# Turning the corner blocks of an attention on VectorE in 32x32 squares

## The chip, the core and the metric

The kernel runs on one core of one Trainium2 chip. What counts is the device time of one execution, in microseconds. Before the change the median of three runs was 533.24 us (532.93 to 533.34). A core has several engines, each with its own queue of instructions that it works through in order: TensorE (matrix products and full transposes; PE in the profile, PEld for its weight loads), VectorE (DVE), ScalarE (ACT), GpSimd (POOL) and SyncE (SP, which here only issues DMA transfers). They wait for each other through semaphores.

## The reference

One layer of an encoder on a sequence of 512 positions of 1024 numbers, all in float32. Cut to what matters:

```python
h = rms_norm(x, attn_norm_g)
xr, gate, q, k, v = split(h @ w_in)
y_rnn  = (rg_lru(conv(xr), forward) + rg_lru(conv(xr), backward)) * gelu(gate)
y_attn = dilated_attention(q, k, v, rel_bias)      # 8 heads of 64
x = x + concat(rms_norm(y_rnn), rms_norm(y_attn)) @ w_out
x = x + square(relu(rms_norm(x) @ w_up)) @ w_down  # 4096 wide
return rms_norm(x, final_norm_g)
```

The attention has three windows per head: 64 keys to each side at distance 1, 64 at distance 4 and 64 at distance 16, each key with a bias by its relative position; the three outputs are weighted by their softmax denominators, which makes it one softmax in which a key counts as often as windows hold it. A query sees keys at most 64 away if the distance is odd or even without being a multiple of four, and up to 256 or 512 away at multiples of four and sixteen. So between positions of different parity only the near keys count.

## The kernel before, in words

**Layout.** Positions are sorted by parity: 256 even ones, then 256 odd ones, in tiles of 128. A query tile needs 256 keys of its own parity and 160 of the other, 416 keys (`NK`) in one contiguous stretch of a doubled key tile `kk`. The scores of a query tile and a head stand in a buffer `e` of 128 queries by 512 columns, of which 416 are in use: columns 0 to 415 for the tiles called far, 96 to 511 for the others. So in each `e` three blocks of 128 keys are full and the fourth holds only 32 keys, those nearest to the border of the tile; the remaining 96 columns are filled with zeros (L840). Of those 32 keys only the 32 queries at that border see any; for the other 96 queries the bias drives the exponential to zero.

**The loop (L1164).** It has five turns `i` and in each four steps `u`, one for each query tile in the order `QSEQ`. Heads go in pairs `p`. In step (i, u) the engines get, in this order:

- `att_s(i, u)` (L815): the scores of pair i, four products on TensorE (L824) into two PSUM banks `ps`;
- `att_t` (L858) for both heads of pair i-1 and the key tile u: four transposes each on TensorE (L862) into a PSUM bank `pt`, then one copy by ScalarE (L864) of 416 of its columns to a buffer `ett` in SBUF. The banks `pt` and the bank `prow` below come from the same two;
- `att_e(i, u)` (L826): for each of the two heads a zero fill by GpSimd (L840), a pass of VectorE that adds the bias and finds the row's minimum (L841), and the exponential with its sum on ScalarE (L842);
- in step 0, `att_z(i-1)`: reciprocals of the sums and a copy to `z` on VectorE (L886, L888). `z` is transposed later in that step by TensorE (`att_zt`, L892, into `prow`) and copied by ScalarE (L893);
- in step 0 of the turns 2 and 4, `att_av` (L955): the products of the transposed exponentials with the values (L964) into `pav`; pair 0 in turn 2, pairs 1 and 2 in turn 4, and pair 3 behind the loop;
- pieces of other work between them: the projections of the next pair's queries and keys (`pqk`, evicted to `qraw` and `kraw`), their splits in a high and a low part (`qh`, `ql`, `kk`; L789, L797, L802), with DMA copies to the other half of the partitions (L791, L799, L803), and the first products of the output projection (`pwo`), from the queue `fillers`; `beside` holds steps at fixed places.

The order on TensorE, ScalarE, VectorE and GpSimd is the order in which the program issues, with no scheduler behind it. Buffers of 128x512 come from one pool of 45 (tag `g`); an instruction that first writes a buffer waits for the last readers of what it held. The bias tiles `tws` (tile `tw`) are loaded by DMA from DRAM two steps and more ahead, into four buffers. Products with weights are made of three passes (L317, L318, L319), of the high and low parts of both factors; ScalarE makes the high part of a weight (`whi`, L252) and VectorE the low part (`wlo`, L274).

Behind the loop come the rest of the output projection (to about 210 us), the up projection and the down projection of the MLP, and the final norm.

The lines that decide which blocks a key tile has:

```python
def blocks(jt):
    par, hj = jt // 2, jt % 2
    own = [(2 * (1 - par) + a, (P * hj if a else TH + P * hj)) for a in range(2)]
    oth = [(2 * par + a, (TH + P * hj if a else P * hj)) for a in range(2)]
    return (own + oth, slice(0, NK)) if hj else (oth + own, slice(S - NK, S))
```

Each entry is a query tile and the column of `e` at which the block of 128 keys starts. The entry whose block is nearly empty is the first for even key tiles (its keys are columns 96 to 127 of `e`), and the last for odd ones (columns 384 to 415).

Of the kernel before, what the change touches and what calls it, by code (L numbers as in the profile page):

```python
# [17 lines left out]
P = 128  # L18
S = 512
# [19 lines left out]
NK = TH + WN  # L39
# [64 lines left out]
def hybrid_kernel(ctx: ExitStack, tc, xw0, xw, xn, w_in, w_v, w_out, w_up, w_dn, gates, vecs, rel, onehot, fg, out):  # L104
    nc = tc.nc
# [12 lines left out]
    def g_(name, dt=FT, shape=(P, S)):  # L118
        return work.tile(list(shape), dt, name=name, tag="g", bufs=NG)

    def small(name, w):
        return work.tile([P, w], FT, name=name, tag="sm%d" % w, bufs=8)

    def ps_(name, tag):
        return psum.tile([P, S], FT, name=name, tag=tag, bufs={"pj": 4, "gs": 2, "et": 2}[tag])
# [361 lines left out]
    def load_tw(h, v):  # L487
        t = work.tile([P, 1024], FT, name="tw", tag="tw", bufs=4)[:, :2 * WN + TH + P]
        b = nbd.offset + h * 2 * S
        nc.sync.dma_start(t[:, WN:WN + TH + P], bass.AP(tensor=nbd.tensor, offset=b, ap=[[1, P], [1, TH + P]]))  # L490
        k = TH - WN - v
        nc.sync.dma_start(bass.AP(tensor=t.tensor, offset=t.offset, ap=[t.ap[0], [WN + TH + P, 2], [1, WN]]),
                          bass.AP(tensor=nbd.tensor, offset=b + S + k, ap=[[1, P], [P - 1 + v - k, 2], [1, WN]]))
        tws[h, v] = t
# [222 lines left out]
    for n, (k, tt) in enumerate(steps):  # L717
        c = C_V + k // 2
# [88 lines left out]
    et, en, zs = {}, {}, {}  # L807
# [7 lines left out]
    def att_s(p, u):  # L815
        qt = QSEQ[u]
        par, far = QT[qt]
        c0 = P * qt
        w = {(0, 0): TH + TH - WN, (0, 1): 0, (1, 0): TH - WN, (1, 1): TH}[par, far]
        psq[p] = [ps_("ps", "gs") for _ in range(2)]  # L820
        for e in range(2):
            k = k_tile(p, e)[:, w:w + NK]
            for i, n in enumerate(("h", "l")):
                nc.tensor.matmul(psq[p][e][:, :NK], lhsT=sp[p, 0, n, e][:, c0:c0 + P], rhs=k, start=i == 0, stop=i == 1)  # L824

    def att_e(p, u):  # L826
        qt = QSEQ[u]
        par, far = QT[qt]
        v = int(par != far)
        if u == 0:  # L830
            en[2 * p], en[2 * p + 1] = {}, {}
            zs[p] = small("zz", 8)
        pss = psq.pop(p)
        c0 = (WN + P) * far
        for e in range(2):
            h = 2 * p + e
            t = g_("e")
            mn = small("mn", 1)
            x = t[:, :NK] if far else t[:, S - NK:]
            nc.gpsimd.memset(t[:, NK:] if far else t[:, :S - NK], 0.0)  # L840
            nc.vector.tensor_tensor_reduce(x, pss[e][:, :NK], tws[h, v][:, c0:c0 + NK], 1.0, 3.0e38, OP.add, OP.min, mn)  # L841
            act(x, x, AF.Exp, scale=-1.0, bias=mn, accum_out=zs[p][:, 2 * qt + e:2 * qt + e + 1])  # L842
            en[h][qt] = t
            if u in (1, 3):
                del tws[h, v]
        if u == 3:
            for e in range(2):
                del sp[p, 0, "h", e], sp[p, 0, "l", e], sp[p, 1, "h", e]
            del kks[p]
# [7 lines that stand above are left out]

    def att_t(h, jt):  # L858
        pt = ps_("pt", "et")
        bs, c = blocks(jt)  # L860
        for i, (qt, k) in enumerate(bs):
            nc.tensor.transpose(pt[:, i * P:(i + 1) * P], en[h][qt][:, k:k + P], ident)  # L862
        t = g_("ett")
        act(t[:, c], pt[:, c], AF.Copy)  # L864
        et[h, jt] = t
        if jt == 3:
            del en[h]

# [15 lines left out]
    def att_z(p):  # L884
        rz = small("rz", 8)
        nc.vector.reciprocal(rz, zs.pop(p))  # L886
        z16[p] = g_("z16")[:, :P]
        nc.vector.tensor_copy(z16[p], fan(rz, 0, 8, 16))  # L888

    def att_zt(p):  # L890
        pr = ps_("prow", "et")
        nc.tensor.transpose(pr[:, :P], z16[p], ident)  # L892
        act(z16[p], pr[:, :P], AF.Copy)  # L893

    def att_zd(p):
        zrow[p] = g_("zrow")
        t = z16.pop(p)
        for qt in range(4):
            r = t[32 * qt:32 * qt + 32]
            nc.sync.dma_start(zrow[p][:, qt * P:(qt + 1) * P],  # L900
                              bass.AP(tensor=r.tensor, offset=r.offset, ap=[r.ap[0], [0, 4], [1, P]]))

    def att_y(p):
        y_add(1)
# [50 lines left out]
    def att_av(p, jts):  # L955
        if 0 in jts:
            pav[p] = ps_("pav", "gs" if p else "pj")
        for jt in jts:
            parts = av_parts(jt)
            for i, (ci, co) in enumerate(parts):  # L960
                for e in range(2):
                    a = slice(64 * e, 64 * e + 64)
                    h = 2 * p + e
                    nc.tensor.matmul(pav[p][a, co], lhsT=vs[:, jt, h * DH:(h + 1) * DH], rhs=et[h, jt][:, ci],  # L964
                                     start=jt == 0 and i == 0, stop=jt == 3 and i == len(parts) - 1, skip_group_check=True)
            for e in range(2):
                del et[2 * p + e, jt]
        if 3 in jts:
            y = g_("yp")
            nc.vector.tensor_tensor(y[:, ::-1], pav.pop(p), zrow.pop(p), op=OP.mult)  # L970
            yat[p] = y
            if p == 3:
                att_a(p)
            if p != 2:
                att_q(p)
            if p < 2:
                att_a(p)
# [64 lines left out]
    def fill(n):  # L1042
        for _ in range(n):
            if fillers and fillers[0] is None:
                fillers.popleft()
                load_x()
            if fillers:
                fillers.popleft()()
# [8 lines left out]
    def add_x():  # L1057
        for fn in more.popleft() if more else ():
            fn()
# [83 lines left out]
    def beside(*key):  # L1143
        for e in plan.pop(key, ()):
            e()
# [18 lines left out]
    for i in range(5):  # L1164
        for u in range(4):
            if i < 4:
                att_s(i, u)
                if u == 2 and i < 3 or u == 0 and i:
                    for e in range(2):
                        load_tw(2 * (i + u // 2) + e, u // 2)  # L1170
            if i >= 1:
                att_t(2 * i - 2, u)
                att_t(2 * i - 1, u)
            if i < 4:
                att_e(i, u)
            if u == 0 and i >= 1:
                att_z(i - 1)
            if u == 0:
                for p in AVS.get(i, ()):
                    att_av(p, range(4))  # L1180
            beside(i, u, 0)
            fill(FILL.get((i, u), (1, 1, 1, 1))[0])
            beside(i, u, 1)
            fill(FILL.get((i, u), (1, 1, 1, 1))[1])
            if u == 1 and i >= 1:
                att_zd(i - 1)
            if u == 0:
                for p in AVS.get(i, ()):
                    if p != 2:
                        att_y(p)  # L1190
            beside(i, u, 2)
            fill(FILL.get((i, u), (1, 1, 1, 1))[2])
            beside(i, u, 3)
            if u == 0 and i >= 1:
                att_zt(i - 1)
            fill(FILL.get((i, u), (1, 1, 1, 1))[3])
            add_x()
            beside(i, u, 4)
# [77 lines left out]
    for w in OSEQ:  # L1276
        for i in range(4):
            tt, k = i // 2, i % 2
# [554 lines left out]
```

## Time and profile before

| what | value |
|---|---|
| median of the runs | 533.24 us |
| time of the profiled execution | 533.13 us |
| its span, first to last instruction | 531.4 us |
| instructions | 8385 |
| TensorE busy | 524.4 us, 3035 products |
| VectorE busy | 434.3 us |
| ScalarE busy | 358.4 us |
| GpSimd busy | 71.7 us |
| transposes L862 | 128, first at 110.2, last at 176.7 us |
| zero fills L840 | 32, of 178 ns |

The profile is of one execution. A row of a group gives the line, the engine, the operation, what is written and read, shapes, the count, and then busy time, mean duration and the idle time of the engine ahead of it with what ended most of it. A row of a timeline gives start, duration and the instruction, with the idle time ahead of it and its releaser in brackets; consecutive equal instructions are merged (x8). The chain follows the work that ended last back through what released each piece. A wait for several things is put down to the one that came last by the profile; where the engine named had long been done, it was another, often a DMA. Durations of TensorE's products overlap, so the distance from start to start is what one costs.

### The profile page before, as it was taken

How to read it: one execution, taken by the hardware profiler on the slowest of the kernel's cores; microseconds unless marked ns; L12 is line 12 of the kernel's file. 1: busy time of each engine (PE TensorE's matmuls, PEld its weight loads, DVE VectorE, ACT ScalarE, POOL GpSimd, SP SyncE). 2: the span in 40 equal slices, each digit the busy share in tenths (PEclk: the TensorE clock that was granted, in tenths of full speed). 3: DMA queues.
4: the chain of work that ended last, by engine and by line, in shares of the span. 5: the costliest groups of instructions: out<-in, count | busy, mean ns of one | idle time of the engine just before them, and what ended most of it. 6: DMA issues, size and time to landing. Idle time of an engine off the chain costs nothing.

```text
span 531.4 us, 8385 instructions
## 1 busy us (share of the span) xinstructions
PE 524.4 (99%) x3035; PEld 452.3 (85%) x3035; DVE 434.3 (82%) x640; ACT 358.4 (67%) x578; POOL 71.7 (13%) x121
## 2 busy tenths in 40 slices
PE   9999999999999999999999999999999999999995
PEld 8857888887887778899999888888999999888884
DVE  6899888986885889799769986879745988986985
ACT  7578955888865756586577755565556786655664
POOL 0282000000100051001110213001001110131000
PEclk9999999999999999999999999999999999999998
DMA  7654386588597279938495899995878397799804
GB/s 284 225 152 134 92 232 185 152 240 214 121 309 263 61 143 201 382 145 202 120 209 152 219 264 275 307 312 132 274 229 212 113 214 209 173 288 263 193 1 159
DMA packets 42602, 107.05 MB, mean 201 GB/s; under 512 B 4916, under 2 KB 15284, under 8 KB 42560
## 3 DMA queue, kind: packets, MB, share of 16 engines
q1 hardware_dynamic: 34848, 80.14, 45.8%
q0 software_dynamic: 7536, 26.14, 26.6%
q8 instruction: 24, 0.39, 0.3%
q10 hardware_dynamic: 176, 0.23, 0.1%
q14 instruction: 18, 0.15, 0.1%
HBM read 94.92 MB, written 4.23 MB: 187 GB/s over the span
## 4 chain that ended last, share of the span: by engine, by line
PE 86%; DVE 5%; ACT 4%; DMA 2%; issue 2%; SPq 0%; DVEq 0%; ACTq 0%
PE pu L318 10%; PE pu L317 10%; PE pu L319 10%; PE pd L317 10%; PE pd L318 9%; PE pd L319 9%; PE pwo L317 3%; PE pt L862 3%; PE pwo L319 3%; PE pwo L318 3%; PE pav L964 2%; PE ps L824 2%; DVE wlo L274 1%; PE pg L538 1%; PE pqk L317 1%
## 5 line engine op out<-in xcount | busy, mean ns | idle before, releaser
L274 DVE TENSOR_TENSOR wlo<-wraw,whi 128x1024 fp32r<-128x1024 f32 x71 | 86.6, 1220 | 23.3 <-ACT whi L252 23.1
L252 ACT ACTIVATE whi<-wraw 128x1024 fp32r<-128x1024 f32 x67 | 70.8, 1058 | 34.9 <-PE pd L319 18.2
L318 PE MATMUL pd<-wlo,ah 128*128 128x512 f32 (+1 forms) x195 | 75.2, 386 | 0.0
L317 PE MATMUL pd<-whi,ah 128*128 128x512 f32 (+1 forms) x195 | 75.2, 386 | 0.0
L319 PE MATMUL pd<-whi,al 128*128 128x512 f32 (+1 forms) x195 | 75.2, 386 | 0.0
L252 ACT ACTIVATE whi<-tw 128x1024 fp32r<-128x1024 f32 x38 | 40.1, 1059 | 40.6 <-DMA tw<-in_w_up_dram 13.2
L318 PE MATMUL pu<-hl,whi 128*128 128x256 f32 x224 | 63.4, 283 | 0.0
L319 PE MATMUL pu<-hh,wlo 128*128 128x256 f32 x224 | 63.4, 283 | 0.0
L317 PE MATMUL pu<-hh,whi 128*128 128x256 f32 x224 | 63.4, 283 | 0.0
L274 DVE TENSOR_TENSOR wlo<-tw,whi 128x1024 fp32r<-128x1024 f32 x38 | 46.4, 1221 | 18.9 <-ACT whi L252 18.9
L317 PE MATMUL pu<-h2h,whi 128*128 128x256 f32 (+1 forms) x200 | 60.1, 300 | 0.0
L318 PE MATMUL pu<-h2l,whi 128*128 128x256 f32 (+1 forms) x200 | 60.0, 300 | 0.0
L319 PE MATMUL pu<-h2h,wlo 128*128 128x256 f32 (+1 forms) x200 | 60.0, 300 | 0.0
L317 PEld LDWEIGHTS pu<-hh,whi 128*128 128x128 f32 x224 | 43.0, 192 | 0.0
L318 PEld LDWEIGHTS pu<-hl,whi 128*128 128x128 f32 x224 | 43.0, 192 | 0.0
L319 PEld LDWEIGHTS pu<-hh,wlo 128*128 128x128 f32 x224 | 43.0, 192 | 0.0
L252 ACT ACTIVATE whi<-ts 128x1024 fp32r<-128x1024 f32 x24 | 25.5, 1061 | 26.0 <-PE pd L319 18.6
L319 PEld LDWEIGHTS pd<-whi,al 128*128 128x128 f32 x195 | 36.6, 188 | 7.4
L317 PEld LDWEIGHTS pd<-whi,ah 128*128 128x128 f32 x195 | 36.6, 188 | 7.3
L318 PEld LDWEIGHTS pd<-wlo,ah 128*128 128x128 f32 x195 | 36.6, 188 | 7.3
L317 PEld LDWEIGHTS pu<-h2h,whi 128*128 128x128 f32 x200 | 38.3, 191 | 1.3
L319 PEld LDWEIGHTS pu<-h2h,wlo 128*128 128x128 f32 x200 | 38.3, 191 | 1.3
(282 smaller groups left out, 1259.1 us busy)
## 6 DMA issues: line engine op xcount, KB each, us to landing
wraw<-in_w_up_dram SPq DMA_DIRECT2D x25, 512.0 KB, 5.6
ts<-in_w_dn_dram POOLq DMA_DIRECT2D x24, 512.0 KB, 13.4
wraw<-in_w_dn_dram SPq DMA_DIRECT2D x24, 512.0 KB, 6.7
tw<-in_w_up_dram SPq DMA_DIRECT2D x15, 512.0 KB, 6.2
tw<-in_w_up_dram POOLq DMA_DIRECT2D x15, 512.0 KB, 8.3
wraw<-in_w_in_dram SPq DMA_DIRECT2D x13, 512.0 KB, 3.7
ts<-in_w_dn_dram SPq DMA_DIRECT2D x8, 512.0 KB, 7.5
tw<-in_w_dn_dram SPq DMA_DIRECT2D x8, 512.0 KB, 6.6
```

Of the source, the lines that this page charges most:

```text
L252: act(hi, raws[i], AF.Copy)
L274: nc.vector.tensor_tensor(lo, r, f(splits[i][0]), op=OP.subtract)
L317: nc.tensor.matmul(o, lhsT=a[0], rhs=b[0], start=bool(first), stop=False, skip_group_check=on)
L318: nc.tensor.matmul(o, lhsT=a[0], rhs=b[1], start=False, stop=False, skip_group_check=on)
L319: nc.tensor.matmul(o, lhsT=a[1], rhs=b[0], start=False, stop=bool(last), skip_group_check=on)
L538: nc.tensor.matmul(pg[2 * d + j][halves[b ^ d]], lhsT=gwr[t][halves[b], c], rhs=xc[t][halves[b]], start=True, stop=True)
L824: nc.tensor.matmul(psq[p][e][:, :NK], lhsT=sp[p, 0, n, e][:, c0:c0 + P], rhs=k, start=i == 0, stop=i == 1)
L862: nc.tensor.transpose(pt[:, i * P:(i + 1) * P], en[h][qt][:, k:k + P], ident)
L964: nc.tensor.matmul(pav[p][a, co], lhsT=vs[:, jt, h * DH:(h + 1) * DH], rhs=et[h, jt][:, ci], start=jt == 0 and i == 0, stop=jt == 3 and i ...
```

## The change

The nearly empty block of each key tile is no longer transposed by TensorE. VectorE's transpose instruction turns 32x32 squares within groups of 32 partitions; a piece of 128 partitions by 32 columns thus becomes four such squares, each in its own partitions. For the 32 columns at the border this is what is wanted: the square of the 32 border queries is the corner block, and the three other squares are zero, since the bias has driven them to zero. `att_t` keeps the three full blocks and copies their 384 columns; the new `att_c` writes the missing 32 columns of the same buffer. It is issued behind `att_e` of the same step, for both heads, and ahead of `att_z`. The zero fills are gone, as nothing reads the 96 columns any longer.

```diff
@@ att_e
             x = t[:, :NK] if far else t[:, S - NK:]
-            nc.gpsimd.memset(t[:, NK:] if far else t[:, :S - NK], 0.0)
             nc.vector.tensor_tensor_reduce(x, pss[e][:, :NK], tws[h, v][:, c0:c0 + NK], 1.0, 3.0e38, OP.add, OP.min, mn)
@@
     def att_t(h, jt):
         pt = ps_("pt", "et")
-        bs, c = blocks(jt)
-        for i, (qt, k) in enumerate(bs):
+        bs = list(enumerate(blocks(jt)[0]))
+        bs.pop(3 if jt % 2 else 0)
+        for i, (qt, k) in bs:
             nc.tensor.transpose(pt[:, i * P:(i + 1) * P], en[h][qt][:, k:k + P], ident)
-        t = g_("ett")
+        t = et[h, jt] = g_("ett")
+        c = slice(bs[0][0] * P, (bs[2][0] + 1) * P)
         act(t[:, c], pt[:, c], AF.Copy)
-        et[h, jt] = t
+
+    def att_c(h, jt):
+        hj = jt % 2
+        qt = blocks(jt)[0][3 if hj else 0][0]
+        c = slice(NK - 32, NK) if hj else slice(S - NK, S - NK + 32)
+        nc.vector.transpose(et[h, jt][:, c], en[h][qt][:, c])
         if jt == 3:
             del en[h]
@@ the loop
             if i < 4:
                 att_e(i, u)
+            if i >= 1:
+                att_c(2 * i - 2, u)
+                att_c(2 * i - 1, u)
             if u == 0 and i >= 1:
                 att_z(i - 1)
```

## The prediction

> **What bounds the kernel now.** I read the page first, then the busy time by stage, then the chain of work that ended last, and last the timelines of the places where that chain leaves TensorE. The page:
>
> ```profile
> span 531.4 us, 8385 instructions
> ...
> PE 524.4 (99%) x3035; PEld 452.3 (85%) x3035; DVE 434.3 (82%) x640; ACT 358.4 (67%) x578; POOL 71.7 (13%) x121
> ...
> PE 86%; DVE 5%; ACT 4%; DMA 2%; issue 2%; SPq 0%; DVEq 0%; ACTq 0%
> ```
>
> A busy PE is not yet a bound, so the stages (first column: the stretch, then its length, then busy us by engine; the attention products to be changed lie in 110 to 182):
>
> ```profile
> core 0: us, PE busy (x) PEld busy (x) DVE busy (x) ACT busy (x) POOL busy (x), PEclk, DMA share, GB/s
> 110.00:116.00 6.00, 5.97 (x35) 4.93 (x35) 4.44 (x13) 4.36 (x10) 0.36 (x2) 1.00 0.94 288
> 116.00:129.00 13.00, 13.00 (x73) 11.34 (x72) 10.11 (x21) 11.55 (x27) 0.36 (x2) 1.00 0.85 198
> 129.00:150.00 21.00, 21.00 (x125) 17.16 (x124) 16.34 (x37) 15.96 (x35) 2.91 (x13) 1.00 0.65 168
> 150.00:164.00 14.00, 14.00 (x81) 12.23 (x80) 9.52 (x22) 9.49 (x26) 0.36 (x2) 1.00 0.93 314
> 164.00:182.00 18.00, 18.00 (x129) 12.39 (x128) 12.43 (x22) 11.51 (x24) 0.00 (x0) 1.00 0.49 167
> 182.00:240.00 58.00, 58.00 (x307) 49.17 (x306) 51.15 (x85) 38.32 (x65) 8.59 (x9) 1.00 0.72 201
> ```
>
> TensorE has no gap from 116 to 240, and the granted clock is full; VectorE is busy for 52.84 and ScalarE for 52.87 of the 72 us of the changed stage (73%). The chain of work shows the changed instructions themselves. Four of the sixteen turns at which the eight transposes stand (pieces: start, us, what):
>
> ```profile
> 110.49 0.87 PE pt L862 x8
> ...
> 115.15 1.03 PE pt L862 x8
> ...
> 172.17 1.09 PE pt L862 x8
> ...
> 176.21 0.87 PE pt L862 x8
> ```
>
> Eight transposes take 0.87 us of the chain, 0.109 us each; two turns are longer by 0.16 and 0.22, where something else ends last. Before 110 no transpose of this kind runs, so nothing of the saving can lie there.
>
> **The change part by part.** I call (i, u) the step u of the turn i of the loop at L1164; the changed products run in i = 1 to 4.
>
> *TensorE.* Each key tile loses one of four transposes: 8 heads by 4 key tiles, 32 of 128.
>
> ```profile
> L862 PEld LDWEIGHTS pt<-ident,e x128: 138/141/146, 110.2 to 176.7; 128*128 128x128 f32 x128
> L862 PE MATMUL pt<-ident,e x128: 270/272/331, 110.3 to 176.8; 128*128 128x128 f32 x128
> ```
>
> The duration of one is 272 ns, but they overlap: the chain's 0.109 us is what one is worth, so 32 x 0.109 = 3.48 us at most. The page "TensorE: Matmul & The Clock Gate" of the Trainium skill, in "Part 4: PE-mode transpose", gives about 275 ns for a transpose in a kernel's context, dominated by access latency; the duration column agrees (272 ns), and the spacing of eight in 0.87 us does not let that be the price. Taken as a price it would make 32 x 0.272 = 8.70 us, a rival below.
>
> *ScalarE and GpSimd.*
>
> ```profile
> L864 ACT ACTIVATE ett<-pt x32: 493/517/519, 111.0 to 177.2; 128x416 f32<-128x416 f32 x32
> L840 POOL MEMSET e<- x32: 168/178/662, 50.4 to 160.8; 128x96 f32 x32
> ```
>
> The eviction shrinks from 416 to 384 columns: by proportion at most 517 x 32/416 = 40 ns each, on an engine that is idle for 19 us of the 72 and not in the chain there. I count nothing. The 32 fills end on GpSimd, 32 x 0.178 = 5.7 us off an engine that is busy for 4 of the 72 us, fills included. I count nothing for them either; the wait for a free buffer that they shared is one that the VectorE instruction behind them has already, on the same buffer.
>
> *VectorE: 32 new transposes of 128x32.* No row shows one. The nearest rows are a smaller and a larger instruction with one input (mean ns behind the comma):
>
> ```profile
> L160 DVE TENSOR_SCALAR z<-e 128x8 f32<-128x8 f32 x1 | 0.2, 161 | 0.0
> ...
> L888 DVE COPY z<-rz 128x128 f32<-128x128 f32 x4 | 0.9, 227 | 0.3
> ```
>
> So it lasts between 161 and 227 ns, near 174 by columns, or 5.6 us in all. What it delays its successor by is less: the copy that starts at 113.01 (below) has its successor start at 113.16, 0.15 us. I take 0.15 us each, 0.30 for the two of a step; the ends are 0.09 (174 less the overlap of 77 that this copy shows) and 0.227. They could be hidden entirely in the 19.2 us in which VectorE is idle between 110 and 182, except where VectorE is itself what TensorE waits for. "VectorE: DVE Perf Modes" of the Trainium skill, "The three transpose paths", gives 311 ns for a bf16 transpose of 128x128 in 32x32 blocks, against 390 for TensorE; no run here shows it. With 311 ns for each of the small ones the sum below would gain 2.31 us instead of 2.63.
>
> *Where VectorE is on the path: the head of pair 1.*
>
> ```profile
> 112.27 0.59 DVE L841 CUSTOM_DVE_ANT_0 e<-ps,tw 128x416 f32<-128x416 f32 x1 [1.49 <-PE pt L862]
> 112.78 0.20 DVE L886 RECIPROCAL rz<-zz 128x8 f32<-128x8 f32 x1
> 113.01 0.23 DVE L888 COPY z<-rz 128x128 f32<-128x128 f32 x1
> 113.16 0.68 DVE L769 SCALAR_TENSOR_TENSOR qraw<-pqk,rrow 128x512 f32<-128x512 f32 x1
> 113.36 0.14 PEld L892 LDWEIGHTS prow<-ident,z 128*128 128x128 f32 x1 [0.35 <-issue]
> 113.87 1.29 ACT L789 ACTIVATE qh<-qraw 64x512 fp32r<-64x512 f32 x2 [0.24 <-DVE qraw L769]
> 115.19 0.28 ACT L893 ACTIVATE z<-prow 128x128 f32<-128x128 f32 x1
> 115.52 0.42 PEld L862 LDWEIGHTS pt<-ident,e 128*128 128x128 f32 x4 [0.17 <-ACT z L893]
> ```
>
> L841 waits 1.49 us. The transposes it names had ended at 111.36 in the chain, so by elimination it waits for its other operand, the bias tile that a DMA brings: its time is fixed. Behind it the new pair of transposes comes before the reciprocal, so the copy z, and with it TensorE's L892, moves 0.30 later, while TensorE arrives 0.22 earlier. In the same way qraw, ScalarE's two qh, and z at 115.19 move 0.30 later, and z frees the PSUM bank in which the second head of step (1,1) is transposed. That group of three then starts at 115.52 + 0.30 and ends 0.109 earlier than four would: TensorE leaves step (1,1) 0.19 late instead of 4 x 0.109 = 0.44 early. Loss 0.63.
>
> *Two more places where the same bank is waited for.*
>
> ```profile
> 136.21 0.98 PEld L862 LDWEIGHTS pt<-ident,e 128*128 128x128 f32 x8
> ...
> 136.40 0.28 ACT L893 ACTIVATE z<-prow 128x128 f32<-128x128 f32 x1
> ...
> 172.60 0.42 PEld L862 LDWEIGHTS pt<-ident,e 128*128 128x128 f32 x4 [0.23 <-ACT z L893]
> ```
>
> At (2,1) z ends at 136.68, and the fifth transpose would start after four of 0.109 behind 136.2, about 136.7: no slack. At (4,1) it waits already. There the first head's saved transpose turns into a longer wait: 2 x 0.109 = 0.22 lost.
>
> *Where the new waits are covered.* The products L964 now wait for VectorE as well. What else queues behind the new transposes on VectorE is the split of K, on which the next pair's scores depend:
>
> ```profile
> 123.73 0.59 DVE L841 CUSTOM_DVE_ANT_0 e<-ps,tw 128x416 f32<-128x416 f32 x1 [1.06 <-PE ps L824]
> ...
> 124.87 1.40 DVE L797 TENSOR_TENSOR kk<-kraw,kk 64x512 fp32r<-64x512 f32 x2
> ...
> 127.29 0.19 PEld L824 LDWEIGHTS ps<-kk,qh 128*128 128x128 f32 x1
> ...
> 176.74 0.42 DVE L925 TENSOR_TENSOR ol<-at,oh 128x256 fp32r<-128x256 f32 x1
> ...
> 178.47 2.95 PE pav L964 x24
> ```
>
> The six transposes of (1,0) to (1,2) add 0.90, which the 1.06 of idle time at 123.73 takes up; the two of (1,3) move the end of kk from 126.27 to 126.57, and TensorE asks at 127.29 less 0.25, so 0.47 remains. In the last turn the transposes of (4,3) stand behind 176.74: done by 177.16 + 4 x 0.15 = 177.8, and the last quarter of the 24 products starts near 178.47 + 2.2 = 180.7. With these covers gone each microsecond would be TensorE's.
>
> *After 182* TensorE runs without a gap, and all that feeds it is issued behind its own or VectorE's steps, so the rest moves as a whole. **Sum:** 3.48 - 0.63 - 0.22 = 2.63 us gain; with 0.09 us for a transpose 2.75, with 0.227 2.48. The profiled execution took 533.13 us (0.11 under the median of the three runs, 533.24, which I leave uncorrected): 533.13 - 2.63 = **530.5 us**.
>
> **The rivals.**
> *All of it is kept.* The bias tile of pair 1 lands earlier, or the new transposes cost VectorE next to nothing: 533.13 - 3.48 = 529.65. For it: the wait at 112.27 is a DMA's, in a stretch with a DMA share of 0.94, and may move. Against: the two waits for z come from program order.
> *VectorE's transposes are dear*, as dear as a pass over 416 columns (0.585, L841's duration here). At the head the loss is then 0.33 + 1.17 = 1.50 instead of 0.63, gain 1.76, 531.4; and as six of them add 3.5 to the 1.06 of idle time, kk ends at 126.27 + 2.4 + 1.2 = 129.9 where TensorE asks for its second half near 128.3: 1.6 lost again, 533.0. Between 531.4 and 533.0. Against it: no row with so few columns is over 227 ns.
> *The saved time returns as waits* (the change does not do what it says): ScalarE's exponentials and VectorE's steps pace the loop, TensorE waits for them, 533.1. For it: both are near 75% busy and feed each other. Against: the gapless rows.
> *Slower: the copy of the split queries.* The transfer that copies ql to the other partitions is issued behind VectorE's split, which moves later, and TensorE asks earlier.
>
> ```profile
> 103.99 6.00 DMA ql<-ql
> ...
> 117.99 1.11 SPq L803 DMA_DIRECT2D ql<-ql  x2
> ```
>
> Pair 1's took 6.00 us to land and TensorE waited for it at 110.0. Pair 2's is asked for near 127.5, 8.4 us after the second issue at 119.1; four new transposes ahead of it (0.6) and TensorE's 0.25 leave 7.6. Each microsecond of landing above 7.6 is TensorE's, and from 7.6 + 2.63 + 1.07 = 11.3 us on the kernel is slower; at 12 us it takes 534.9.
> *Each transpose is worth its duration*, by the rule weighed above: 533.13 - 8.70 = 524.4; the 0.87 us for eight speak against it.
>
> **How the numbers follow.** The forecast 0.62; all kept 0.15; dear transposes 0.08; returned as waits 0.07; slower 0.07; full duration 0.01. What a measurement can tell from no change is 0.2%, 1.07 us, so up to 532.17 is faster and from 534.31 slower. Faster: 0.62 + 0.15 + 0.01 and half of the dear case, 0.82; same: its other half and the returned waits, 0.11; slower 0.07. The range: below, the kept case with 0.25 of spread, 529.4; above, the edge of "faster" with the cheaper half of the dear case, 532.2: 0.62 + 0.15 + 0.04 = 0.81.
>
> **What would show it.** L862 has 96 instead of 128, in chain pieces of six with 0.65 us; a VectorE group of 32 with 160 to 230 ns; no group L840. In turn 1, L892 stands a little later than 113.4 and the second group of (1,1) near 115.8; from there on every step is 0.22 shorter than before, except (2,1) and (4,1), which show waits for z. From 182 on the same work, 2.6 earlier. It is wrong if L824 at the head of pair 2 or 3 waits for kk or ql, if L964 waits for VectorE, if the gapless rows break after 182, or if the bias tile's wait at 112.27 has another length.

## The result and the profile after

| | before | after |
|---|---|---|
| median of five runs each, one chip | 532.93 us (532.74 to 533.34) | 530.61 us (530.37 to 531.29) |
| profiled execution | 533.13 us, span 531.4 | 530.99 us, span 528.9 |

The changed kernel takes 0.9958 of the time before, with a 95% interval of 0.9943 to 0.9972. A second comparison on another chip (below) gave 530.22 against 533.63 us, 0.9939 (0.9926 to 0.9952). The forecast was 530.5 us.

In the changed kernel the lines have moved a little: the bias pass is L840 (L841 before), the exponential L841, the copy from `pt` to `ett` L865, the new VectorE transposes L871, reciprocal and copy of `z` L892 and L894, the transpose of `z` into `prow` L898, its copy by ScalarE L899, the products with the values L970. The page of the changed kernel has, of busy time by engine and of the chain of work that ended last:

```profile
span 528.9 us, 8275 instructions
...
PE 521.5 (99%) x3003; PEld 448.0 (85%) x3003; DVE 437.5 (83%) x672; ACT 357.2 (68%) x578; POOL 66.0 (12%) x89
...
PE 96%; DMA 1%; DVE 1%; issue 1%; ACT 0%; SPq 0%; DVEq 0%; ACTq 0%
```

TensorE has lost 32 instructions and 2.9 us, VectorE has gained 32 instructions and 3.2 us, GpSimd has lost its 32 fills and 5.7 us. By stage, with the same columns as before:

```profile
110.00:116.00 6.00, 5.65 (x30) 4.28 (x28) 4.64 (x13) 4.07 (x11) 0.00 (x0) 1.00 0.94 291
116.00:129.00 13.00, 12.95 (x70) 11.13 (x69) 10.64 (x29) 11.45 (x27) 0.00 (x0) 1.00 0.83 212
129.00:150.00 21.00, 21.00 (x122) 17.03 (x121) 18.31 (x49) 16.67 (x38) 1.05 (x1) 1.00 0.66 172
150.00:164.00 14.00, 14.00 (x79) 11.79 (x79) 9.96 (x27) 9.30 (x26) 0.00 (x0) 1.00 0.96 320
164.00:182.00 18.00, 17.96 (x122) 12.40 (x119) 14.96 (x34) 12.04 (x27) 0.00 (x0) 1.00 0.46 154
182.00:240.00 58.00, 58.00 (x317) 49.63 (x316) 51.04 (x83) 39.07 (x67) 8.61 (x9) 1.00 0.75 209
```

TensorE now has small gaps at the head of pair 1 (0.35 us in the first row, 0.05 in the second) and 0.04 in the last turn; elsewhere it still runs without one. The two groups, transposes of VectorE and of TensorE (minimum, median and maximum of one in ns, then first and last start):

```profile
L871 DVE STREAM_TRANSPOSE ett<-e x32: 167/187/211, 113.2 to 175.3; 128x32 f32<-128x32 f32 x32
...
L862 PE MATMUL pt<-ident,e x96: 270/272/328, 110.7 to 174.4; 128*128 128x128 f32 x96
```

What one turn of the transposes was worth is read from the chain of both kernels. First the kernel before, at four places that the prediction did not show, then the changed one at the same four, at (1,1) and at the end of the last turn (start, length, what):

```profile
119.67 0.87 PE pt L862 x8
...
136.56 0.87 PE pt L862 x8
140.93 0.87 PE pt L862 x8
...
160.92 0.87 PE pt L862 x8
```

```profile
116.09 0.55 PE pt L862 x3
...
120.15 0.66 PE pt L862 x6
...
136.43 0.65 PE pt L862 x6
...
140.60 0.66 PE pt L862 x6
...
159.57 0.66 PE pt L862 x6
...
174.06 0.66 PE pt L862 x6
176.11 2.96 PE pav L970 x24
```

At step (1,2) the changed kernel stands 0.48 us behind the kernel before (120.15 against 119.67), at (3,3) 1.35 us ahead of it (159.57 against 160.92). So nine steps, each with two transposes fewer, gave 1.83 us, 0.203 a step.

The transposes themselves gave a little more. The timeline of TensorE at (1,2), first before, then after:

```profile
119.52 1.03 PE L862 MATMUL pt<-ident,e 128*128 128x128 f32 x8
120.31 0.48 PE L317 MATMUL pqk<-h_hi,whi 128*128 128x512 f32 x1
```

```profile
119.99 0.82 PE L862 MATMUL pt<-ident,e 128*128 128x128 f32 x6
120.56 0.48 PE L317 MATMUL pqk<-h_hi,whi 128*128 128x512 f32 x1
```

From the first transpose to the product behind the group it is 0.790 us before and 0.572 after (to the nanosecond of the trace), so two transposes were worth 0.218, 0.109 each. The other 0.015 of a step went into the products between the groups: over the nine steps they take 33.96 us before and 34.10 after. In e2 below, which keeps all of TensorE's transposes, they take 34.07, and in e1, which has none on VectorE, 34.10. So the longer time comes with either part of the change alone, and the saved transposes are not shown to be its cause; there is one trace of the kernel before, and the cause is open.

At the last products with the values (176.11 against 178.47) it is 2.36 us ahead, and keeps that to the end: from there the rest takes 352.95 us before and 352.89 after.

That the changed kernel stood behind at first is not shown to be an effect of the change. The first score product of pair 1 starts at 109.20 us before and at 109.77 after; over all traces of this study it lies between 108.5 and 110.2, and the versions differ ahead of it in little more than the fills of pair 0 (109.2 to 109.5 in the three that have them). From that product to the last products with the values it is 69.20 us before and 66.28 after: **2.92 us gained in the stage**, of which the late start takes 0.57 in this pair of executions.

At the head of pair 1, in the timeline of VectorE, ScalarE and TensorE's weight loads of the changed kernel:

```profile
112.65 0.59 DVE L840 CUSTOM_DVE_ANT_0 e<-ps,tw 128x416 f32<-128x416 f32 x1 [1.29 <-issue]
113.16 0.30 DVE L871 STREAM_TRANSPOSE ett<-e 128x32 f32<-128x32 f32 x2
113.39 0.16 DVE L892 RECIPROCAL rz<-zz 128x8 f32<-128x8 f32 x1
113.58 0.23 DVE L894 COPY z<-rz 128x128 f32<-128x128 f32 x1
113.72 0.68 DVE L769 SCALAR_TENSOR_TENSOR qraw<-pqk,rrow 128x512 f32<-128x512 f32 x1
113.92 0.14 PEld L898 LDWEIGHTS prow<-ident,z 128*128 128x128 f32 x1 [0.76 <-issue]
114.44 1.29 ACT L789 ACTIVATE qh<-qraw 64x512 fp32r<-64x512 f32 x2 [0.42 <-DVE qraw L769]
115.76 0.28 ACT L899 ACTIVATE z<-prow 128x128 f32<-128x128 f32 x1
116.08 0.31 PEld L862 LDWEIGHTS pt<-ident,e 128*128 128x128 f32 x3 [0.28 <-ACT z L899]
```

The chain of the prediction is all there: the bias pass waits, the two transposes stand between it and the reciprocal, L898 waits for the copy of `z`, the second group of transposes of (1,1) for ScalarE's copy of `z`. The pair of transposes holds the reciprocal up by 0.23 us from their own start.

### The profile page after: what moved, and what is told of

Its sections match the earlier page's. It is cut to its first block, busy times and chain, and to the rows that moved or that the text cites. A ratio compares the mean times of both kernels' runs of the same rounds, so it can differ in the third digit from the quotient of the medians.

```text
span 528.9 us, 8275 instructions
## 1 busy us (share of the span) xinstructions
PE 521.5 (99%) x3003; PEld 448.0 (85%) x3003; DVE 437.5 (83%) x672; ACT 357.2 (68%) x578; POOL 66.0 (12%) x89
## 3 DMA queue, kind: packets, MB, share of 16 engines
HBM read 94.92 MB, written 4.23 MB: 187 GB/s over the span
## 4 chain that ended last, share of the span: by engine, by line
PE 96%; DMA 1%; DVE 1%; issue 1%; ACT 0%; SPq 0%; DVEq 0%; ACTq 0%
PE pu L317 10%; PE pu L318 10%; PE pu L319 10%; PE pd L317 10%; PE pd L318 10%; PE pd L319 10%; PE pwo L317 3%; PE pqk L317 3%; PE pwo L319 3%; PE pwo L318 3%; PE pqk L319 3%; PE pqk L318 3%; PE pav L970 2%; PE ps L824 2%; PE pt L862 2%; PE pv L317 2%
## 5 line engine op out<-in xcount | busy, mean ns | idle before, releaser
L252 ACT ACTIVATE whi<-wraw 128x1024 fp32r<-128x1024 f32 x67 | 70.8, 1059 | 36.5 <-PE pd L319 19.3
L252 ACT ACTIVATE whi<-tw 128x1024 fp32r<-128x1024 f32 x38 | 40.2, 1059 | 40.7 <-DMA tw<-in_w_up_dram 12.9
L252 ACT ACTIVATE whi<-ts 128x1024 fp32r<-128x1024 f32 x24 | 25.5, 1061 | 23.9 <-PE pd L319 18.1
```

The lines of the kernel that those rows point to most:

```text
L252: act(hi, raws[i], AF.Copy)
```

## The experiments

Two of the quantities that the versions below are compared by have to be told apart, because one of them varies by itself. The bias pass at the head waits for the transfer of pair 1's second bias tile; the trace records the end of that wait, and it lies between 2.11 and 3.21 us behind the first score product of pair 1 (2.26 to 3.21 among versions with the same instructions ahead of it). I take this end as the landing; the last completion that the trace has of that transfer lies 0.03 us ahead of it in all fourteen traces. So I give, all in us: the landing, the start of `z`'s copy on VectorE and of L898 (all behind the first score product of pair 1), the stage (from there to the last products with the values), what of the stage lies behind L898, and what of it lies behind the landing.

| version | landing | copy `z` | L898 | stage | behind L898 | behind landing |
|---|---|---|---|---|---|---|
| before | 2.99 | 3.82 | 4.19 | 69.20 | 65.01 | 66.22 |
| after | 2.79 | 3.81 | 4.19 | 66.28 | 62.09 | 63.48 |
| e9, the change again | 2.70 | 3.72 | 4.09 | 66.14 | 62.05 | 63.44 |
| e1, zeros by GpSimd | 3.00 | 3.83 | 4.20 | 66.28 | 62.08 | 63.28 |
| e2, VectorE's part added | 2.83 | 4.00 | 4.38 | 69.48 | 65.11 | 66.65 |
| e3, corner first | 2.99 | 4.20 | 4.57 | 66.64 | 62.07 | 63.65 |
| e4, fills kept | 2.11 | 3.13 | 3.51 | 65.61 | 62.10 | 63.50 |
| e5, corner twice | 3.15 | 4.66 | 5.04 | 68.28 | 63.24 | 65.13 |
| e6, other bank | 3.21 | 4.23 | 4.51 | 66.20 | 61.69 | 62.99 |
| e7, later place | 2.26 | 3.28 | 4.20 | 67.51 | 63.32 | 65.25 |
| e8, all three | 3.09 | 4.31 | 4.69 | 65.58 | 60.89 | 62.48 |
| e10, all three again | 3.01 | 4.23 | 4.53 | 65.50 | 60.97 | 62.50 |
| e11, corner first, other bank | 3.04 | 4.25 | 4.53 | 66.06 | 61.53 | 63.02 |
| e12, other bank, later place | 3.12 | 4.14 | 4.71 | 65.58 | 60.87 | 62.46 |

The runs e1 to e4 share one chip (the kernel before: 533.24 us there), e5 to e8 another (533.6), e9 to e11 a third (533.63), and e12 ran by itself (533.46).

**TensorE's part alone.** The corner is not turned; GpSimd writes zeros where it would stand.

```diff
-        nc.vector.transpose(et[h, jt][:, c], en[h][qt][:, c])
+        nc.gpsimd.memset(et[h, jt][:, c], 0.0)
```

> The 32 columns of the corner block are filled with zeros by GpSimd instead of being turned by VectorE, so the corner's part of the attention is left out; TensorE's part of the change stands alone. I measure the attention stage from the first L824 of step (1,0) to the first value product of pair 3 (69.20 us before: 109.20 to 178.40; 66.27 with the change: 109.77 to 176.04). My theory: the head of pair 1 hangs on the bias tile and on VectorE's chain behind it, so even without a VectorE transpose about 0.33 us of the 3.48 are lost there and 0.1 at (4,1); without the two transposes' delay the stage is 0.2 shorter than with the change, 66.0 to 66.1, and the time about 530.4. Rival, all of the loss is VectorE's transposes: the stage is 65.7 (69.20 less 3.48), the time 530.0. Rival, nothing hangs on VectorE: the stage stays at 66.3.

Measured: 530.92 us, ratio 0.9954 (0.9940 to 0.9968), and a stage of 66.28, as long as the change's: above what was expected. The landing explains it: it came 0.21 later than in the trace of the change. From the landing this version needs 63.28 against 63.48, so VectorE's transposes cost the change 0.2 us, and behind L898 nothing at all (62.08 against 62.09).

**VectorE's part alone.** The kernel before, with the 32 transposes added behind `att_e`, into a buffer that nobody reads.

```diff
+            if i >= 1:
+                att_c(2 * i - 2, u)      # nc.vector.transpose(spare[:, :32], en[h][qt][:, c])
+                att_c(2 * i - 1, u)
```

> The kernel before, with its four TensorE transposes and its fills, and the 32 VectorE transposes added beside them at the place where the change has them, into a spare tile that nobody reads: VectorE's part alone. My theory: only the head of pair 1 feels it, L892 and the second group of (1,1) start 0.23 later (two transposes of 0.115); the stage is 69.4 to 69.5 us, the time 0.2 above the kernel before, which a measurement can't tell from it. Rival, VectorE paces the loop: 32 x 0.115 = 3.7 us appear, the stage is up to 72.9 and the time up to 536.6.

Measured: 533.51 us, ratio 1.0004 (0.9994 to 1.0014), and a stage of 69.48. The groups of this version, with mean ns and idle time behind the bars:

```profile
L871 DVE STREAM_TRANSPOSE spare<-e 128x32 f32<-128x32 f32 x32 | 6.7, 209 | 0.6
```

6.7 us more work on VectorE cost the stage 0.28 us, which is what was expected, but with luck: the landing came 0.16 earlier. From the landing it is 0.43 (66.65 against 66.22), 0.34 up to L899, this version's transpose of `z`, where 0.23 was expected, and some 0.1 behind it (65.11 against 65.01). All 32 transposes write the same buffer here; the pair at the head lasts 0.46 us, against 0.30 in the change, so this version overstates what they cost there. VectorE does not pace the loop, or 3.7 us would have appeared; that ScalarE does not either is seen from the stage of the change, which kept most of what it saved.

**The corner ahead of the bias passes.** The two calls of `att_c` stand ahead of `att_e(i, u)`, so that no transpose lies between the waiting pass and `z`.

```diff
+            if i >= 1:
+                att_c(2 * i - 2, u)
+                att_c(2 * i - 1, u)
             if i < 4:
                 att_e(i, u)
-            if i >= 1:
-                att_c(2 * i - 2, u)
-                att_c(2 * i - 1, u)
```

> The changed kernel with the VectorE transposes issued ahead of the bias pass of the same step instead of behind it. In step (1,0) they then stand in the time in which VectorE waits for the bias tile. My theory: L898 and the second group of (1,1) come 0.23 earlier, the stage is 66.0 to 66.1 us instead of 66.27, the time 530.4. Rival, the bias passes and the exponentials behind them are what paces the loop: every bias pass comes 0.23 later and the stage is longer than 66.3.

Measured: 530.6 us, ratio 0.9952 (0.9935 to 0.9969), and a stage of 66.64: a miss. The later landing makes 0.19 of it. But from the landing it is 63.65, 0.17 more than in the change, where 0.2 less was expected. VectorE's timeline of this version:

```profile
110.06 0.30 DVE L871 STREAM_TRANSPOSE ett<-e 128x32 f32<-128x32 f32 x2
110.28 0.55 DVE L840 CUSTOM_DVE_ANT_0 e<-ps,tw 128x416 f32<-128x416 f32 x1
...
112.51 0.59 DVE L840 CUSTOM_DVE_ANT_0 e<-ps,tw 128x416 f32<-128x416 f32 x1 [1.67 <-PE pqk L319]
...
113.02 0.20 DVE L892 RECIPROCAL rz<-zz 128x8 f32<-128x8 f32 x1
113.26 0.23 DVE L894 COPY z<-rz 128x128 f32<-128x128 f32 x1
```

From the start of the pass to the copy of `z` it is 0.75 us, as in the kernel before, so the transposes are gone from that piece. But the pass starts at 112.51, and its wait for the bias tile had ended at 112.04: 0.46 us, where it is 0.08 in the change and in all others that don't put the corner ahead of the pass. The TensorE product that the row names is not what the pass needs: of TensorE it asks only for its own scores, which stand far ahead of that product. The same 0.46 to 0.47 us show in the three other traces with the corner first (e8, e10, e11). In the four the named product ends 0.06 to 0.13 us ahead of the pass: the pass keeps its distance from the landing, not from that product. The saving of 0.19 was eaten twice over.

**The fills put back.**

```diff
             x = t[:, :NK] if far else t[:, S - NK:]
+            nc.gpsimd.memset(t[:, NK:] if far else t[:, :S - NK], 0.0)
```

> The changed kernel with the 32 zero fills put back on GpSimd; nothing reads what they write. My theory: they cost nothing, the stage is 66.3 us within 0.1 and the time that of the changed kernel, 530.6 within 0.5. Rival, the fills were in somebody's way (their buffers, or the SBUF beside VectorE): the stage is longer by some part of 32 x 0.178 = 5.7 us.

Measured: 530.49 us, ratio 0.9946 (0.9926 to 0.9966), stage 65.61, 0.6 below what was expected. All of it is the landing, at 2.11 the earliest of the study: from there it is 63.50 against 63.48, and behind L898 62.10 against 62.09. The fills were free, and their removal brought nothing.

**The corner turned twice.** The transpose of VectorE is written down twice.

```diff
         nc.vector.transpose(et[h, jt][:, c], en[h][qt][:, c])
+        nc.vector.transpose(et[h, jt][:, c], en[h][qt][:, c])
```

> The changed kernel with each VectorE transpose issued twice, into the same columns: 64 instead of 32. I measure the stage behind the bias tile's landing, from the second bias pass of (1,0) to the first value product of pair 3, as the landing itself moved between 2.19 and 3.45 us behind the first L824 of pair 1 in the runs so far (with the change: 63.40 behind a pass at 2.88). My theory: z is copied 0.19 later (two more transposes) and the stage behind the landing is 0.2 longer, 63.6. Rival, VectorE paces the loop: 32 x 0.115 = 3.7 longer, 67.1.

Measured: a single execution, 532.74 us, and from the landing 65.13: 1.65 more than the change, between the two theories. At the head the copy of `z` starts 1.51 behind the landing instead of 1.02. The rest comes from two other places; the first is step (2,1), in the timeline of TensorE's weight loads:

```profile
136.99 0.31 PEld L862 LDWEIGHTS pt<-ident,e 128*128 128x128 f32 x3 [0.32 <-DVE cs L440]
138.01 0.31 PEld L862 LDWEIGHTS pt<-ident,e 128*128 128x128 f32 x3 [0.71 <-ACT z L900]
```

In the change six transposes of this step run through without a gap. Here both groups wait, and by the starts of the score products (135.87 and 140.93 us, in the change 135.29 and 139.47) the step is 0.88 longer. The rest arises at (4,0), where two pieces of the transposes wait for ScalarE's exponentials (0.24 and 0.31 us idle). A doubled cost at VectorE is thus worth 0.49 at the head, but 1.65 in all: at (2,1) VectorE has a slack that one pair of transposes a step does not use up and two do (it is followed to its source below, in the account of the prediction).

**`prow` in the bank of another tag.** `z` is transposed into the bank that the projections use, so that the transposes of (1,1) need not wait for its copy.

```diff
-        pr = ps_("prow", "et")
+        pr = ps_("prow", "pj")
```

> The changed kernel with the bank of prow taken from the four of tag pj instead of the two that the transposes use. My theory: the second head's transposes at (1,1) and (4,1) no longer wait for ScalarE's copy of z, 0.21 and 0.20 us; the stage from L898 of turn 1 to the first value product of pair 3, 62.09 with the change, becomes 61.7, the time 530.2. Rival, other waits take their place (the projections' banks are one fewer): 62.1 or more.

Measured: 530.18 us, ratio 0.9946 (0.9930 to 0.9963), behind L898 61.69. TensorE's weight loads at (1,1), (4,0) and (4,1) in this version:

```profile
113.27 0.14 PEld L898 LDWEIGHTS prow<-ident,z 128*128 128x128 f32 x1 [0.66 <-DVE z L894]
...
114.70 0.76 PEld L862 LDWEIGHTS pt<-ident,e 128*128 128x128 f32 x6
...
162.40 0.20 PEld L862 LDWEIGHTS pt<-ident,e 128*128 128x128 f32 x2 [0.19 <-ACT e L841]
...
171.26 0.81 PEld L862 LDWEIGHTS pt<-ident,e 128*128 128x128 f32 x6
```

Both waits for ScalarE's copy of `z` are gone, the six transposes of those steps run without one, and 0.40 us are gained behind L898, 0.49 from the landing. The other 0.09 lie at L898 itself, which starts 0.28 us behind the copy of `z` by VectorE here and 0.37 in the change. The rival holds in part: at (4,0) a new wait for an exponential (0.19 us idle at the line of 162.40) cost 0.18 of what had been gained by then. The chain from `qraw` over two `qh` and `z` to the bank was the cause of the wait at (1,1).

**The transpose of `z` a quarter of the fillers later.**

```diff
-            if u == 0 and i >= 1:
-                att_zt(i - 1)
             fill(FILL.get((i, u), (1, 1, 1, 1))[3])
+            if u == 0 and i >= 1:
+                att_zt(i - 1)
```

> The changed kernel with the transposition of z (L898) issued one piece of filler work later on TensorE, three products of 0.23, in its old bank. My theory: TensorE no longer waits for z at L898, but the bank of the second head at (1,1) is still freed by the chain that begins with the bias tile (bias pass, qraw, two qh, copy of z on ScalarE), so those transposes still start 3.1 us behind the second bias pass of (1,0) and nothing is gained: the stage from that pass stays 63.4. Rival, the wait at L898 is what costs: the stage is 0.4 to 0.5 shorter, 62.9.

Measured: a single execution, 532.44 us, stage 67.51: a clear miss. The wait at L898 went, as expected, but L898's successors paid more. ScalarE and TensorE's weight loads of this version:

```profile
114.32 1.29 ACT L789 ACTIVATE qh<-qraw 64x512 fp32r<-64x512 f32 x2 [0.42 <-DVE qraw L769]
115.64 1.06 ACT L252 ACTIVATE whi<-wraw 128x1024 fp32r<-128x1024 f32 x1
116.60 0.26 ACT L899 ACTIVATE z<-prow 128x128 f32<-128x128 f32 x1
...
116.91 0.31 PEld L862 LDWEIGHTS pt<-ident,e 128*128 128x128 f32 x3 [1.42 <-ACT z L899]
```

The filler past which the step was moved also issues the next weight's conversion on ScalarE (L252, 1.06 us). Now this stands ahead of the copy of `z`, and the bank comes free that much later. At (2,1) the same happens, with a wait of 0.91 us; from the landing this version needs 1.77 us more than the change. A step that is moved past another is moved past all that the other issues, on every queue.

**All three.** Corner first, `prow` in the other bank, and the later place, which in that bank holds nobody up.

> All three together: VectorE transposes ahead of the bias pass, L898 one piece of filler work later, its bank from pj. My theory: TensorE no longer waits at L898, at (1,1) and at (4,1), and the landing of the bias tile is off the path unless it is later than 3.3 us behind the first L824; the stage from there to the first value product of pair 3 is 66.28 - 0.52 - 0.41 = 65.3 to 65.4 us, and the time 0.9 below the changed kernel, 529.7. Rival, what is saved returns as another wait (the queries' copy, the K split, the projections' banks): 66 or more, 530.6.

Measured: 529.99 us, ratio 0.9942 (0.9927 to 0.9956), stage 65.58, 0.70 below the change and 0.2 longer than expected. L898's weight load still waits 0.17 us for `z`.

**Three versions on one chip.** The medians so far lay within each other's intervals and came from different chips, so the change, all three edits, and all three without the later place ran side by side.

> The changed kernel once more, beside the two versions below on one chip, since their times so far (530.61, 530.18 and 529.99 us) come from different chips and lie closer than their intervals. Theory: behind L898 the stretch to the products of pair 3 is 62.1 us again, as in every version with the old bank of prow; only the offset of L898 (4.19 in the first look) moves with the landing of pair 1's bias tile, by up to 0.5. Time 530.6 +- 0.5 us, ratio to the kernel before 0.995 to 0.996.

> Corner turned ahead of the bias passes, prow in its own bank, the transpose of z a quarter of the fillers later, on the same chip as the change. Theory: the remaining loss of the change sits in the wait for z's copy and in the bank of prow, so this one is 0.4 to 0.9 us under the change (60.9 us behind L898, with L898 about 0.5 later): 529.7 to 530.2 us. Rival: the 0.6 us between the two medians came from chips and starts: then it is within 0.2 us of the change.

> As the run above, but the transpose of z stays where it was. Theory: the later place is only worth something when the bias tile lands late, since it hides the wait at L898. So behind L898 61.7 us as with the other bank alone, and L898 0.75 + 0.37 us behind the start of the second bias pass (0.19 less than in the change): stage 0.5 to 0.6 us under the change at the same landing of the tile, 530.0 us, and 0 to 0.5 us over the run above. Rival: the move alone carries the gain, and this one equals the change.

Measured: the change 530.22 us (ratio 0.9939, 0.9926 to 0.9952), all three edits 529.64 (0.9927, 0.9915 to 0.9939), without the later place 530.26 (0.9942, 0.9930 to 0.9954). The profiles say more than the medians: the change needs 63.44 from the landing, as before; the other bank 63.02, as in e6 (62.99), which is 0.4 less than the change where 0.5 to 0.6 was expected; with the later place as well 62.50, as in e8. So each edit but "corner first" shortened the stage, by about half a microsecond each, the later place only together with the other bank, and did so again. In the run times it doesn't separate: e10 is 0.58 us under the change, but their intervals overlap, and e11, whose traced landing was 0.35 later than that of e9, equals the change.

**The corner behind the passes again, with the other two edits.**

```diff
-        pr = ps_("prow", "et")
+        pr = ps_("prow", "pj")
@@ the loop
-            if u == 0 and i >= 1:
-                att_zt(i - 1)
             fill(FILL.get((i, u), (1, 1, 1, 1))[3])
+            if u == 0 and i >= 1:
+                att_zt(i - 1)
```

> As the version with all three edits, but the corner is turned behind the bias passes again, as in the change. In all four looks with the corner first, the second bias pass of (1,0) began 0.46 to 0.47 us behind the end of its wait for the bias tile; in the nine others 0.08 to 0.11. Theory: that delay comes with the order of VectorE's instructions. So here it is 0.1 again, the copy z starts 1.02 behind the landing instead of 1.21, L898 no longer waits the 0.2 that it waited for z, and from the landing to the products of pair 3 it takes 62.3 us (62.5 with the corner first; 63.5 in the change): 529.5 us, if the tile lands near 3.0. Rival: the delay belongs to something else, as to where L898 stands: then it is 0.46 here as well, and the stretch from the landing is 62.7 or more, since the turns at VectorE come on top.

Measured: 529.97 us, ratio 0.9939 (0.9925 to 0.9953). The pass started 0.08 behind the landing and the copy of `z` 1.02 behind it, as the theory has it; so the delay of 0.46 comes with the order. The stretch from the landing was 62.46, not 62.3: L898 no longer waits for `z` at all, and so what came before it on TensorE decides, a wait for the split queries that in this execution was longer than in e10 (0.64 idle against 0.46). Behind that wait TensorE's products run without a gap, so the tile's landing no longer sets this stage.

```profile
109.93 0.19 PEld L824 LDWEIGHTS ps<-kk,ql 128*128 128x128 f32 x1 [0.64 <-DMA ql<-ql]
```

e8, e10 and e12 are one result within what these runs can tell: about 0.7 us off the change's stage, and medians of 529.6 to 530.0 us.

## Why the prediction was right, and where only its sum was

The sum was 3.48 - 0.63 - 0.22 = 2.63 us. It assumed the bias tile to land at a fixed time behind the first score product, and is therefore to be held against the stretch behind the landing: 66.22 - 63.48 = **2.74 us** (2.77 and 2.72 with e9 and e4). The prediction had named another length of that wait as a sign that it is wrong; the wait was 1.29 us instead of 1.49, and the landing alone made that. Its terms:

*TensorE, 3.48.* Right: a transpose that is left out was worth the 0.109 us that lie from start to start, and sixteen groups that are shorter by 0.218 make 3.49. But 0.19 of it did not arrive, as the products between the groups took longer (0.14 of this by the nine steps from (1,2) to (3,3)); no term of the prediction had that, and its cause is open. That the duration of 272 ns is no price is shown: 32 times that would have been 8.70. The 275 ns that the page "TensorE: Matmul & The Clock Gate" of the Trainium skill has in its "Part 4: PE-mode transpose" agree with the duration.

*The head of pair 1, 0.63.* The mechanism was right in each link, and e6 took the bank's part away. Its size was 0.33 for the transposes of TensorE that fall into waits and 0.30 for two on VectorE. The second part measured 0.19 (1.02 against 0.83 from the landing to the copy of `z`; without VectorE's transposes e1 has 0.83 as well). So 0.15 each was too much; it is 0.095 in this place, at the lower end that the prediction gives (174 less 77 is 97 ns, which it writes as 0.09). By TensorE's own times the term is 0.51: it leaves step (1,1) 0.08 later behind the landing than before, and would have left it 0.44 earlier. "VectorE: DVE Perf Modes" of the Trainium skill ("The three transpose paths") has no shape as small as this: its 311 ns are for bf16 and 128x128, and 128x32 in float32 took 187 here. The rival that has VectorE's transposes as dear as a pass of 585 ns is out by the 187 ns and by the 0.19 at the head.

*Steps (2,1) and (4,1), 0.22.* Wrong for (2,1): from its transposes to those of (2,2) it is 4.37 us before (136.56 to 140.93) and 4.17 after (136.43 to 140.60), so the step kept its whole 0.20. The copy of `z` ended at 136.43 in the changed kernel, and the fourth of six weight loads from 136.08 on was due at about that time. What stands ahead of that copy, in VectorE's and ScalarE's timelines, first before, then after:

```profile
132.38 0.69 DVE L970 TENSOR_TENSOR yp<-pav,zrow 128x512 f32<-128x512 f32 x1 [1.48 <-PE pav L964]
...
135.09 1.28 ACT L789 ACTIVATE qh<-qraw 64x512 fp32r<-64x512 f32 x2 [0.68 <-DVE qraw L769]
```

```profile
132.19 0.69 DVE L976 TENSOR_TENSOR yp<-pav,zrow 128x512 f32<-128x512 f32 x1 [0.57 <-DMA tw<-nbd]
...
134.84 1.28 ACT L789 ACTIVATE qh<-qraw 64x512 fp32r<-64x512 f32 x2 [0.68 <-DVE qraw L769]
...
136.08 0.76 PEld L862 LDWEIGHTS pt<-ident,e 128*128 128x128 f32 x6
136.15 0.28 ACT L899 ACTIVATE z<-prow 128x128 f32<-128x128 f32 x1
```

The prediction held `z` at its old time while TensorE came earlier. But ScalarE copies `z` right behind `qh`, `qh` waits for `qraw`, VectorE makes `qraw` behind `yp`, and `yp` takes up TensorE's products with the values, whose last one ends at 132.27 before and at 132.15 after (0.04 ahead of `yp`, whose row names a transfer). TensorE came earlier there too, and so did `z` (136.15 against 136.40). How near the edge it is, e5 shows: the 1.48 us for which VectorE idles ahead of `yp` before are 0.57 in the change and nothing in e5, where `yp` starts 0.95 behind the last of those products and `z` keeps the transposes waiting. At (4,1) the wait grew from 0.23 to 0.28 us, some 0.05 lost instead of 0.109:

```profile
170.76 0.31 PEld L862 LDWEIGHTS pt<-ident,e 128*128 128x128 f32 x3 [0.28 <-ACT z L899]
```

Together: 3.49 - 0.51 - 0.05 - 0.19 = 2.74, as measured. Both losses of the prediction were too large, by 0.12 and 0.17 us; a loss of 0.19 that it did not have made up for two thirds of this, by luck. The forecast was nearer than its steps deserved.

*What was put at nothing.* GpSimd's fills: e4 and the change agree within 0.02 behind the landing. ScalarE's shorter copy lasted 486 ns (median) instead of 517; no run has it alone. The cover of `kk`, and the rival of the late copy of the split queries: L824 at the heads of pairs 2 and 3 has no wait for either. L970 waited for no transpose in the change; in e5 the profile puts the wait at the last ones down to VectorE's transpose, with the same 0.36 us idle as in the change. The rest behind pair 3 moved as a whole, 352.95 against 352.89.

*From the stage to the time.* The two profiled executions differ by 2.14 us, made of the 2.74, 0.19 for a landing that happened to be earlier, -0.57 for a later start, 0.06 behind pair 3, and -0.28 outside the span. The rival "all kept" named the tile's landing as what could move; it did move, by up to 1.1 us between executions, but VectorE's transposes cost their 0.19 whenever it landed. The medians' difference, 2.32, and that on the other chip, 3.41, lie on both sides of 2.74.

## What to carry to other kernels

Price an instruction that is removed from a gapless engine by the distance from start to start, never by its duration, and check it by the shift that equal steps show between two traces, which can be a little less; and let everything that hangs on the shortened engine move with it, as here `z` did at (2,1). Before a version's time is explained, look for a transfer that lands at another time in every execution, and compare versions from that landing on. A step that is moved in program order moves past everything that the skipped piece issues, on all engines.

## What the runs showed that was not expected

The second bias tile of pair 1 landed between 2.11 and 3.21 us behind the first score product, in a stretch with a DMA share of 0.94 before and after; these 1.1 us are two fifths of what the change gains.

Two VectorE transposes ahead of a bias pass delayed the second pass, which had long waited for its transfer, by 0.38 us more than the wait itself (0.46 to 0.47 us from the end of the wait to the start in four traces of four; 0.08 in ten of ten without). The two passes have the same waits in both orders. What makes the delay is open: it follows the order of the instructions (e12), but no run separated why.

In step (3,3) ScalarE sat idle for 2.12 us ahead of its copy to `ett`. The transposes that it copies had ended at 159.90 us; behind that it waited for a buffer whose last reader was a transfer, until 160.49. Before the change the same wait had ended at 160.52, when the transposes were still running (to 161.36). So the time that is saved runs into a transfer here. TensorE was not held up by it in the change; the new wait of e6 at (4,0) comes behind it, where ScalarE's exponentials follow that copy.

```profile
160.69 0.88 ACT L865 ACTIVATE ett<-pt 128x384 f32<-128x384 f32 x2 [2.12 <-DMA zrow<-z]
```
